# Turning the RWKV-7 recurrence's operands token-major: VectorE 32x32 block transposes in place of TensorE transposes through PSUM

## The chip, the cores and the metric

One Trainium2 chip, one core. The metric is the device time of the whole program in microseconds; three runs of the kernel before gave a median of 3381.07 us (3380.14 to 3383.0).

## What is computed

One decoder layer over 16 meta tokens and 2048 tokens of width 1024: a norm, one input projection, then two mixers side by side (sliding-window attention and an RWKV-7 recurrence), a gated merge, an output projection, and a SwiGLU feed-forward part. The change touches the recurrence alone. Cut to that:

```python
def step(S, inp):                       # per token, per head, state S is 64 x 64
    r_t, w_t, k_t, v_t, a_t, b_t = inp
    sa = einsum('bhvk,bhk->bhv', S, a_t)
    S = S * w_t[:, :, None, :] + sa[..., None] * b_t[:, :, None, :] + v_t[..., None] * k_t[:, :, None, :]
    y = einsum('bhvk,bhk->bhv', S, r_t)
    return S, y
```

The kernel computes this in chunks of 64 tokens, with the triangular system inside a chunk inverted.

## The kernel before, in words

**Two streams, one TensorE order.** The dense work is a generator: phase a (the input projection, 4 blocks of 512 tokens, 37 column chunks each) and then phase c for each block (branch projections `pb`, output projection `ph_o`, feed-forward products `pg`, `pu`, `ph_d`). Every product takes three matmul passes of 128x512 per 128 rows (`mm3`, a high and a low part of each operand). The mixers are generators too (`attn`, `lora`, `rwkv`). `tick()` advances one kind of mixer after every 4/3 us of dense work by a fixed credit, so each mixer moves one `yield` per 4 us of credit. `InOrder` (lines 82 to 98) ties all TensorE instructions to the order in which this loop writes them. On the other engines a scheduler places instructions by a timeline model; those of the dense part go through `High` (lines 191 to 206) and so take precedence. Three PSUM buffers (`psd`) serve the dense products, four (`psg`) the mixers, one (`psc`) the recurrence.

**One round of the recurrence.** `rwkv(i, j)` does 256 tokens (4 chunks) of 2 heads; there are 8 x 4 rounds and one more for the meta tokens, 33 in all. In order:
- The inputs are shifted into `rkv` (L562): r, k and v, feature-major. TensorE makes `pa` and `pz`; VectorE takes `rnb` (L679) and `kp` from `pa`.
- VectorE writes `bkd` (L730, L731): b and k of the four chunks, block-diagonal by head, 128 features by 128 (head, token). `bkd` has one buffer.
- TensorE multiplies `bkd` by `ar` into `pg` (this name is also used by the feed-forward gate; the mixer's is 128x128), VectorE masks it into `g` (L750, L756, L758).
- `g` goes through DRAM (`lt_d`) to GpSimd, which inverts the 32x32 blocks in 31 steps (L772, L774) into `xv`; that goes back through DRAM (`xt_d`) into `td`.
- Beside that inversion, L777 to L796 turn b, k (`bkd`) and v token-major: eight TensorE transposes into `pb`, two ScalarE copies into `bt`; two TensorE transposes of v into `pvv`, two VectorE and two ScalarE copies into the block-diagonal `vd`. (`pb` is also the name of the branch projections' PSUM tiles.)
- After `WAIT_INV` = 9 further yields `td` is read; VectorE turns its lower blocks (`tq`, L808, the kernel's only use of VectorE's transpose), and the four chunks run one after the other in the PSUM tile `ch`, with `vd`, `bt`, `ud` (L840), `rd` and the state `sd` (L845).

Up to three rounds are under way at once; a new one starts every 14 yields.

Of the kernel before, what the change touches and what calls it, by code (L numbers as in the profile page):

```python
# [19 lines left out]
F32 = mybir.dt.float32  # L20
F32R = mybir.dt.float32r
AF = mybir.ActivationFunctionType
# [5 lines left out]
P = 128  # L28
# [19 lines left out]
WAIT_INV = 9  # L48
# [30 lines left out]
def layer(ctx, tc, x, meta, w_in, w_br, w_o, w_gate, w_up, w_down, w2a, a2, g2, vecs, sinks, gfin,  # L79
          consts, rope, out):  # L80
    nc = tc.nc
    V, A, G, S = nc.vector, nc.scalar, nc.gpsimd, nc.sync
# [18 lines left out]
    T = InOrder()  # L101
# [8 lines left out]
    cp = pool("const")  # L110
    dp = pool("dram", space=DRAM)
    dn = pool("dense")
    mx = pool("mixer")
    psd = pool("psd", bufs=3, space=PSUM)
    psg = pool("psg", bufs=4, space=PSUM)
# [26 lines left out]
    ident = cc("ident")  # L142
# [407 lines left out]
    bkd = cp.tile([P, 2, 4, P], F32, name="bkd")  # L550
    vds = [cp.tile([P, 4, P], F32, name=f"vd{q}") for q in range(2)]
    td = cp.tile([P, 4, P], F32, name="td")
    rd = cp.tile([P, P], F32, name="rd")
    ud = cp.tile([P, P], F32, name="ud")
    for t in (bkd, *vds, td, rd):
        G.memset(t, 0.0)
    gmask = cst[:, _CC["gstrict"][0]:_CC["gincl"][1]]

# [56 lines left out]
    n = TU // CH  # L615

    def rwkv(i, j):
# [3 lines left out]
        m = i is None  # L621
        uid = 4 * NU if m else 4 * i + j
        nm = f"{i}_{j}"
        t1 = lambda s, b=1: mx.tile([P, TU], F32, tag=s, bufs=b, name=f"{s}_{nm}")
        cv = lambda ap: ap.rearrange("p (c t) -> p c t", t=CH)
# [17 lines left out]
        rm, km, vm = (rkv[:, q] for q in range(3))  # L643
# [84 lines left out]
        for h in range(2):  # L728
            hb = slice(64 * h, 64 * h + 64)
# [13 lines left out]
        for x in range(2):  # L743
            pg = psg.tile([P, 512], F32, tag="pg", name=f"pg_{nm}_{x}")
# [29 lines left out]
            G.tensor_add(xv[:, :, r + 1:], xv[:, :, r + 1:], pr[:, :, :n_])  # L774
        yield

        bt = mx.tile([P, 2, n, P], F32, tag="bt", bufs=2, name=f"bt_{nm}")  # L777
        vd = vds[(uid + m) % 2]
        for x in range(2):
            pb = psg.tile([P, 512], F32, tag="pg", name=f"pb_{nm}_{x}")  # L780
            for c in range(n):
                T.transpose(pb[:, c * P:(c + 1) * P], bkd[:, x, c], ident)
            A.activation(bt[:, x], pb.rearrange("p (c f) -> p c f", f=P), AF.Copy)
            if x == 0:
                yield
        pvv = psg.tile([P, 512], F32, tag="pg", name=f"pvv_{nm}")
        for t in range(2):
            T.transpose(pvv[:, t * P:(t + 1) * P], vm[:, t * P:(t + 1) * P], ident)
        pvt = pvv[:, :2 * P].rearrange("p (t f) -> p t f", f=P)
        for q in range(2):  # L790
            for h in range(2):
                hb, qb = slice(64 * h, 64 * h + 64), slice(64 * q, 64 * q + 64)
                if q == h:
                    V.tensor_copy(vd[hb, q::2, hb], pvt[qb, :, hb])
                else:
                    A.activation(vd[hb, q::2, hb], pvt[qb, :, hb], AF.Copy)  # L796
        for _ in range(WAIT_INV):
            yield
        G.dma_start(xt_d[uid].rearrange("m (b c) i -> b m (c i)", c=4), xv.rearrange("p c i -> p (c i)"))
        lo, hi = [slice(64 * h, 64 * h + 32) for h in range(2)], [slice(64 * h + 32, 64 * h + 64) for h in range(2)]  # L800
# [23 lines left out]
        for c in range(n):  # L824
# [8 lines left out]
            for h in range(2):  # L833
                hb = slice(64 * h, 64 * h + 64)
# [192 lines left out]
    def tick():  # L1027

        turn[0] = (turn[0] + 1) % TURNS
        rs = [u for u in units if u[2] == "r"]  # L1030
        for u in list(units):
            if turn[0] != (0 if u[2] == "a" else 1 if len(rs) > 1 and u is rs[0] else 2):
                continue
            u[1] += 1
            if next(u[0], 0) == 0:
                units.remove(u)
        if todo_r and turn[0] == 2:
            i, j = todo_r[0]
            b = (i or 0) // 2
            young = min((u[1] for u in units if u[2] == "r"), default=LAG)  # L1040
            if young >= LAG - 3 and i not in asked and set(range(6, 9)) <= emitted[b]:
                asked.add(i)
                start("l", lora(i), b)
            if young >= LAG and i in loras and set(
                    range(9, 21) if i is None else range(PAIR0 + 3 * j, PAIR0 + 3 * j + 3)) <= emitted[b]:
                todo_r.pop(0)
                start("r", rwkv(i, j), b)
        if todo_a and turn[0] == 0 and not any(u[2] == "a" for u in units):
            ti = todo_a[0]
            b = (ti or 0) // 4  # L1050
            if set(range(6)) <= emitted[b]:
                todo_a.pop(0)
                start("a", attn_meta() if ti is None else attn(ti), b)
# [135 lines left out]
```

## Time and profile before

| what | value |
|---|---|
| median of three runs | 3381.07 us |
| the profiled execution's own time | 3377.94 us |
| its span, first to last instruction | 3376.0 us |
| TensorE (PE) busy | 3256.3 us, 96% |
| VectorE (DVE) busy | 1542.1 us, 46% |
| ScalarE (ACT) busy | 1163.2 us, 34% |
| GpSimd (POOL) busy | 1156.1 us, 34% |
| mean granted TensorE clock | 0.987 |

The page's busy time is the union of an engine's instructions. The chain that ended last runs through PE for 60% of its span. Stages on the time axis: phase a to about 1150 us, phase c of the first block to about 1810 us, of the second to about 2370 us, of the third to about 2890 us, of the fourth to the end; the recurrence's rounds lie between about 190 and 2880 us. "Phase c" below means these stretches from 1150 us on.

### The profile page before, as it was taken

What the parts mean: (1) busy time and instruction counts of PE and PEld (TensorE: products, weight loads), DVE (VectorE), ACT (ScalarE), POOL (GpSimd) and SP (SyncE); (2) the same over time, 40 slices, a digit from 0 to 9 for tenths busy, and PEclk for the clock granted to TensorE, in tenths of its full rate; (3) what the DMA queues carried; (4) which work ended last, traced back from release to release, by engine and by line L of the source; (5) the groups of instructions that cost most, each with busy time, mean ns of one, the idle gap of its engine ahead of it and who ended that gap; (6) DMA issues with size and microseconds to landing.
All of it is one profiled execution on the core that took longest, in us unless ns stands there. A gap on an engine that the chain in (4) does not pass through costs nothing.

```text
span 3376.0 us, 47237 instructions
## 1 busy us (share of the span) xinstructions
PE 3256.3 (96%) x16909; PEld 2681.2 (79%) x16909; DVE 1542.1 (46%) x3622; ACT 1163.2 (34%) x2863; POOL 1156.1 (34%) x2771
## 2 busy tenths in 40 slices
PE   7899999999999998999999999999999999999998
PEld 6777887787888777887787788887888888778887
DVE  3343233232332585666666644445654443542233
ACT  4354344443443455445443422233242221220001
POOL 1124434334344454554453433444333341000000
PEclk9999999999999999999999999999999999999999
DMA  7777666676666776666668555556755555855555
GB/s 262 273 261 241 209 226 211 190 227 197 223 210 215 242 260 206 234 235 234 231 237 280 176 170 174 179 181 201 263 171 177 171 177 176 288 179 191 196 191 181
DMA packets 229448, 721.46 MB, mean 214 GB/s; under 512 B 36333, under 2 KB 90989, under 8 KB 168286
## 3 DMA queue, kind: packets, MB, share of 16 engines
q1 hardware_dynamic: 158126, 516.15, 47.1%
q0 software_dynamic: 38736, 154.99, 12.9%
q10 hardware_dynamic: 32352, 47.31, 3.8%
q8 instruction: 133, 2.18, 0.3%
q14 instruction: 101, 0.83, 0.1%
HBM read 533.46 MB, written 184.82 MB: 213 GB/s over the span
## 4 chain that ended last, share of the span: by engine, by line
PE 60%; DMA 6%; DVE 3%; POOL 3%; ACT 2%; issue 2%; SPq 0%; POOLq 0%; DVEq 0%; ACTq 0%
PE pg L93 14%; PE pu L93 12%; PE ph_d L93 11%; PE pi L93 6%; PE pb L93 4%; PE ch L93 4%; PE ph_o L93 3%; DMA yl<-y_d 1%; PE ph_o_l L93 1%; POOL pr L772 1%; POOL xv L774 1%; DMA lt<-lt_d 1%; PE py L93 1%; PE pq L93 1%; DVE h L202 1%
## 5 line engine op out<-in xcount | busy, mean ns | idle before, releaser
L93 PE MATMUL pi<-act_u,w_in 128*128 128x512 f32 x3552 | 902.5, 402 | 10.5 <-DVE m L202 6.1
L93 PEld LDWEIGHTS pi<-act_u,w_in 128*128 128x128 f32 x3552 | 652.9, 191 | 144.0 <-issue 5.5
L93 PE MATMUL pg<-act_f,w_g 128*128 128x512 f32 x2112 | 533.7, 399 | 6.8 <-DVE act_f L202 6.8
L93 PE MATMUL pu<-act_f,w_u 128*128 128x512 f32 x2112 | 522.9, 395 | 0.0
L93 PE MATMUL ph_d<-w_d,mg_g 128*128 128x512 f32 x1920 | 472.5, 397 | 10.4 <-DVE h L202 10.0
L93 PEld LDWEIGHTS pg<-act_f,w_g 128*128 128x128 f32 x2112 | 388.4, 189 | 85.3 <-DVE act_f L202 9.0
L93 PEld LDWEIGHTS pu<-act_f,w_u 128*128 128x128 f32 x2112 | 388.9, 188 | 78.8 <-issue 1.0
L93 PEld LDWEIGHTS ph_d<-w_d,mg_g 128*128 128x128 f32 x1920 | 355.5, 189 | 85.9 <-DVE h L202 14.5
L772 POOL TENSOR_TENSOR pr<-xv,lt 128x124 f32<-128x124 f32 (+30 forms) x992 | 330.5, 333 | 248.9 <-DMA lt<-lt_d 176.8
L774 POOL TENSOR_TENSOR xv<-xv,pr 128x124 f32<-128x124 f32 (+30 forms) x992 | 341.1, 344 | 74.5
L202 DVE SCALAR_TENSOR_TENSOR h<-ph_d,h 128x512 f32<-128x512 f32 x320 | 218.9, 689 | 130.0 <-PE ph_d L93 128.3
L93 PE MATMUL pb<-ya,w_br 128*128 128x512 f32 x768 | 191.0, 400 | 1.0 <-DMA w_br<-wd_br 0.6
L93 PEld LDWEIGHTS pb<-ya,w_br 128*128 128x128 f32 x768 | 143.1, 191 | 30.9 <-DVE mg_m L202 1.0
L202 DVE SCALAR_TENSOR_TENSOR th<-th,pg 128x512 f32<-128x512 f32 x88 | 60.4, 687 | 214.6 <-ACT th L202 214.5
L93 PE MATMUL ph_o<-w_o,mg_m 128*128 128x512 f32 x576 | 144.2, 400 | 6.8 <-DVE h L202 3.8
L804 POOL DMA_DIRECT2D td<-xt_d x132 | 72.6, 557 | 225.4 <-PE ch L93 197.3
L202 ACT ACTIVATE th<-pg 128x512 f32<-128x512 f32 x88 | 52.6, 598 | 281.4 <-PE pg L93 281.0
L202 DVE TENSOR_TENSOR th<-th,pu 128x512 f32<-128x512 f32 x88 | 60.5, 687 | 183.8 <-PE pu L93 183.3
L243 POOL TENSOR_TENSOR ss_o<-ss_o,mhalf 128x1 f32<-128x1 f32 x16 | 9.4, 590 | 372.5 <-DVE ss_o L202 372.3
L755 POOL DMA_DIRECT2D lt_d<-g x128 | 71.2, 561 | 184.0 <-DVE g L750 182.0
L202 ACT ACTIVATE mg_g<-th 128x512 fp32r<-128x512 f32 x88 | 55.3, 628 | 222.6 <-DVE th L202 222.5
L93 PEld LDWEIGHTS ph_o<-w_o,mg_m 128*128 128x128 f32 x576 | 106.5, 190 | 31.3 <-DVE h L202 5.2
(356 smaller groups left out, 4512.1 us busy)
## 6 DMA issues: line engine op xcount, KB each, us to landing
w_in<-wd_in SPq DMA_DIRECT2D x111, 1024.0 KB, 5.5
w_g<-wd_g SPq DMA_DIRECT2D x66, 1024.0 KB, 5.0
w_u<-wd_u SPq DMA_DIRECT2D x66, 1024.0 KB, 5.0
w_d<-wd_d SPq DMA_DIRECT2D x60, 1024.0 KB, 5.0
wd_in<-w_in POOLq DMA_DIRECT2D x37, 1024.0 KB, 5.8
w_br<-wd_br SPq DMA_DIRECT2D x24, 1024.0 KB, 7.0
wd_g<-w_g POOLq DMA_DIRECT2D x22, 1024.0 KB, 5.2
wd_u<-w_u POOLq DMA_DIRECT2D x22, 1024.0 KB, 5.3
```

Of the source, the lines that this page charges most:

```text
L93: r = f(*p, **k)
L202: return f(*p, **k)
L243: G.tensor_tensor(ss[:rows, 3:4], ss[:rows, 2:3], mhalf[:rows, 0:1], op=ALU.pow)
L755: G.dma_start(lt_d[uid, m0:m0 + n].rearrange("c j i -> j c i"), g[r32, :, 0, o])
L772: G.tensor_mul(pr[:, :, :n_], xv[:, :, r:r + 1].to_broadcast([P, 4, n_]), lt[:, r, r + 1:].unsqueeze(1).to_broadcast([P, 4, n_]))
L774: G.tensor_add(xv[:, :, r + 1:], xv[:, :, r + 1:], pr[:, :, :n_])
L804: G.dma_start(td[r32, :, r32], xt_d[uid, m0:m0 + 4].rearrange("m j i -> j m i"))
```

## The change

The ten TensorE transposes of a round, its two 128x512 ScalarE copies from PSUM and its four copies of v go. In their place VectorE issues 24 transposes of 32 partitions by 4 blocks of 32, from SBUF straight into SBUF: eight from v into the diagonal blocks of `vd`, sixteen from `bkd` into the diagonal blocks of `bt`. `bt` becomes two fixed tiles that GpSimd zeroes once at the start; it was a rotating pair before, so the space is the same. The number of yields of a round stays: 1 + 9 before, 2 + 8 now. Half of the new transposes (r different from q) write to other partitions than they read.

```diff
-    for t in (bkd, *vds, td, rd):
+    bts = [cp.tile([P, 2, 4, P], F32, name=f"bt{q}") for q in range(2)]
+    for t in (bkd, *vds, td, rd, *bts):
         G.memset(t, 0.0)
...
-        bt = mx.tile([P, 2, n, P], F32, tag="bt", bufs=2, name=f"bt_{nm}")
-        vd = vds[(uid + m) % 2]
+        bt, vd = bts[(uid + m) % 2], vds[(uid + m) % 2]
+        vc4 = cv(vm)
+        for h in range(2):
+            for r in range(2):
+                for q in range(2):
+                    rb, qb = (slice(64 * h + 32 * z, 64 * h + 32 * z + 32) for z in (r, q))
+                    V.transpose(vd[qb, :, rb], vc4[rb, :, 32 * q:32 * q + 32])
         for x in range(2):
-            pb = psg.tile([P, 512], F32, tag="pg", name=f"pb_{nm}_{x}")
-            for c in range(n):
-                T.transpose(pb[:, c * P:(c + 1) * P], bkd[:, x, c], ident)
-            A.activation(bt[:, x], pb.rearrange("p (c f) -> p c f", f=P), AF.Copy)
-            if x == 0:
-                yield
-        pvv = psg.tile([P, 512], F32, tag="pg", name=f"pvv_{nm}")
-        for t in range(2):
-            T.transpose(pvv[:, t * P:(t + 1) * P], vm[:, t * P:(t + 1) * P], ident)
-        pvt = pvv[:, :2 * P].rearrange("p (t f) -> p t f", f=P)
-        for q in range(2):
+            yield
             for h in range(2):
-                hb, qb = slice(64 * h, 64 * h + 64), slice(64 * q, 64 * q + 64)
-                if q == h:
-                    V.tensor_copy(vd[hb, q::2, hb], pvt[qb, :, hb])
-                else:
-                    A.activation(vd[hb, q::2, hb], pvt[qb, :, hb], AF.Copy)
-        for _ in range(WAIT_INV):
+                for r in range(2):
+                    for q in range(2):
+                        rb, qb = (slice(64 * h + 32 * z, 64 * h + 32 * z + 32) for z in (r, q))
+                        V.transpose(bt[qb, x, :, rb], bkd[rb, x, :, qb])
+        for _ in range(WAIT_INV - 1):
             yield
```

**Where the instructions stand, PE.** One round in phase c of the first block, among the passes of an output projection (`ph_o`) and of a branch projection (`pb_6_0`, with `ya` and `w_br`). Before:

```order
L93 MATMUL ph_o_5_1_1_11952<-w_o_5_1_11933,mg_m_3_11374 128x512 x3
L93 MATMUL ch_2_0_11783<-rd,td 128x128
L93 MATMUL pb_3_0_11962<-cst,bkd 128x128 x4
L93 MATMUL ph_o_5_2_1_11969<-w_o_5_1_11933,mg_m_2_11304 128x512 x3
...
L93 MATMUL pb_6_0_12008<-ya_1_11083,w_br_6_11997 128x512 x3
L93 MATMUL pb_3_1_12015<-cst,bkd 128x128 x4
L93 MATMUL pvv_3_12021<-cst,rkv_3_11340 128x128 x2
L93 MATMUL pb_6_0_12008<-ya_2_11089,w_br_6_11997 128x512 x3
```

With the change:

```order
L93 MATMUL ph_o_5_1_1_12004<-w_o_5_1_11985,mg_m_3_11426 128x512 x3
L93 MATMUL ch_2_0_11835<-rd,td 128x128
L93 MATMUL ph_o_5_2_1_12022<-w_o_5_1_11985,mg_m_2_11356 128x512 x3
...
L93 MATMUL pb_6_0_12061<-ya_1_11127,w_br_6_12050 128x512 x3
L93 MATMUL pb_6_0_12061<-ya_2_11133,w_br_6_12050 128x512 x3
```

The ten transposes of the round are gone and everything else stands in its place; the same holds for all 33 rounds, 330 instructions.

**DVE, behind bkd.** The same round, from its last `bkd` product on (`mt`: a branch projection leaves PSUM; `w_br`: low part of a weight; `kw`: attention keys; `gst`: the norm of an earlier round). Before:

```order
L731 TENSOR_TENSOR bkd<-kp_3_11489,pi_3_11635 64x4x64
L202 SCALAR_TENSOR_TENSOR mt_5_0_11670<-tg_5_0_11605,pb_5_0_11620 128x512
L859 TENSOR_REDUCE gst_1_11679<-ysq_1_11683 128x4
L736 TENSOR_TENSOR fc_3_11651<-pe_3_11633 128x3
L822 TENSOR_SCALAR sd_110<-sd_110,pe_2_3_11654 128x128
L885 TENSOR_TENSOR kw<-kl_11744,kw 64x128 x4
L202 SCALAR_TENSOR_TENSOR mt_5_1_11707<-tg_5_1_11607,pb_5_1_11672 128x512
L860 TENSOR_SCALAR gst_1_11679<-gst_1_11679 128x4
L202 TENSOR_TENSOR w_br_6_11997<-wr_br_6_0_11998,w_br_6_11997 128x512
```

With the change:

```order
L737 TENSOR_TENSOR fc_3_11703<-pe_3_11685 128x3
L818 TENSOR_SCALAR sd_110<-sd_110,pe_2_3_11706 128x128
L792 STREAM_TRANSPOSE bt_122<-bkd 32x4x32
L881 TENSOR_TENSOR kw<-kl_11796,kw 64x128 x2
L792 STREAM_TRANSPOSE bt_122<-bkd 32x4x32 x4
L881 TENSOR_TENSOR kw<-kl_11796,kw 64x128 x2
L792 STREAM_TRANSPOSE bt_122<-bkd 32x4x32
L202 SCALAR_TENSOR_TENSOR mt_5_1_11759<-tg_5_1_11659,pb_5_1_11724 128x512
L792 STREAM_TRANSPOSE bt_122<-bkd 32x4x32
L856 TENSOR_SCALAR gst_1_11731<-gst_1_11731 128x4
L792 STREAM_TRANSPOSE bt_122<-bkd 32x4x32
```

The sixteen transposes into `bt` stand right behind `bkd`, between the dense instructions and ahead of `g` (L751 in the changed kernel).

**DVE, behind rkv.** The same round earlier, among the products that add an output projection to `h`. Before:

```order
L202 SCALAR_TENSOR_TENSOR h_11105<-ph_o_3_0_1_11459,h_11105 128x512
L202 TENSOR_TENSOR w_br_5_11609<-wr_br_5_1_11614,w_br_5_11609 128x512
L202 SCALAR_TENSOR_TENSOR h_11105<-ph_o_3_1_1_11467,h_11105 128x512
L679 TENSOR_SCALAR rnb_3_11500<-pa_3_11487 64x2 x4
L602 MEMSET dl_12191 64x256
```

With the change:

```order
L202 SCALAR_TENSOR_TENSOR h_11149<-ph_o_3_0_1_11511,h_11149 128x512
L202 TENSOR_TENSOR w_br_5_11661<-wr_br_5_1_11666,w_br_5_11661 128x512
L785 STREAM_TRANSPOSE vd_117<-rkv_3_11392 32x4x32 x8
L202 SCALAR_TENSOR_TENSOR h_11149<-ph_o_3_1_1_11519,h_11149 128x512
L680 TENSOR_SCALAR rnb_3_11552<-pa_3_11539 64x2 x4
```

The eight transposes into `vd` stand ahead of the sum that frees the next PSUM buffer and ahead of `rnb`; in 28 of the rounds the eight stand together.

## Rows read from the trace of the kernel before

**Rows 1.** The page, part 1: busy us, share of the span, instructions

```profile
PE 3256.3 (96%) x16909; PEld 2681.2 (79%) x16909; DVE 1542.1 (46%) x3622; ACT 1163.2 (34%) x2863; POOL 1156.1 (34%) x2771
```

**Rows 2.** Busy time by stretch: PE, PEld, DVE, ACT, POOL, then clock, DMA share, GB/s

```profile
0.00:1150.00 1150.00, 1093.60 (x5842) 893.12 (x5843) 390.41 (x1164) 482.56 (x1184) 401.17 (x971) 0.98 0.69 226
1150.00:1810.00 660.00, 625.88 (x3296) 509.85 (x3295) 445.32 (x1017) 318.61 (x788) 334.32 (x715) 0.98 0.70 239
1810.00:2370.00 560.00, 552.50 (x2957) 461.14 (x2956) 281.83 (x623) 165.00 (x425) 231.00 (x606) 0.99 0.59 192
2370.00:2890.00 520.00, 515.01 (x2751) 431.13 (x2750) 245.11 (x541) 133.17 (x345) 174.60 (x460) 0.99 0.56 187
```

**Rows 3.** Waits of PE: us in total, times, longest us

```profile
PE psS L93 <- DVE qs L956: 27.3, 9, 5.8
...
PE ph_d L93 <- DVE h L202: 10.0, 7, 4.5
```

**Rows 4.** Timeline of PE, 320 to 328 us: start us, us, instructions

```profile
320.35 1.63 PE L93 MATMUL pi<-act_u,w_in 128*128 128x512 f32 x6
321.82 0.60 PE L93 MATMUL pb<-cst,bkd 128*128 128x128 f32 x4
322.17 3.02 PE L93 MATMUL pi<-act_u,w_in 128*128 128x512 f32 x12
...
325.17 1.63 PE L93 MATMUL pi<-act_u,w_in 128*128 128x512 f32 x6
...
327.07 0.38 PE L93 MATMUL pvv<-cst,rkv 128*128 128x128 f32 x2
327.21 1.17 PE L93 MATMUL pi<-act_u,w_in 128*128 128x512 f32 x4
```

**Rows 5.** The chain that ended last, a dense run without mixers

```profile
3084.14 10.88 PE ph_d L93 x48
```

**Rows 6.** Groups by shape: busy us, mean ns, then idle before and its releaser

```profile
L93 PE MATMUL pb<-cst,bkd 128*128 128x128 f32 x256 | 38.8, 275 | 0.0
...
L783 ACT ACTIVATE bt<-pb 128x512 f32<-128x512 f32 x64 | 38.2, 596 | 120.9 <-PE pb L93 120.9
...
L794 DVE COPY vd<-pvv 64x128 f32<-64x128 f32 x64 | 18.4, 288 | 26.8 <-ACT vd L796 15.1 <-PE pvv L93 10.8
...
L93 PE MATMUL pvv<-cst,rkv 128*128 128x128 f32 x64 | 12.2, 273 | 0.0
```

**Rows 7.** The tile tq: duration ns min/median/max, first and last start

```profile
L808 DVE STREAM_TRANSPOSE tq<-td x64: 289/302/304, 385.0 to 2815.8; 32x128 f32<-32x128 f32 x64
```

**Rows 8.** Timeline of DVE, 459 to 461 us: two transposes in a row

```profile
459.16 0.62 DVE L808 STREAM_TRANSPOSE tq<-td 32x128 f32<-32x128 f32 x2
```

**Rows 9.** DVE busy from bkd's end to g, eight rounds, 1150 to 1810 us

```profile
1213.76:1220.11 6.35, 6.28 (x16) 1.00 0.69 169
...
sum 59.32, DVE 36.77; mean DVE 4.60
```

**Rows 10.** The same, thirteen rounds, 1810 to 2890 us

```profile
sum 94.90, DVE 40.90; mean DVE 3.15
```

**Rows 11.** The same, twelve rounds before 1150 us

```profile
sum 111.01, DVE 22.44; mean DVE 1.87
```

**Rows 12.** Waits of ACT and DVE: us in total, times, longest us

```profile
ACT bt L783 <- PE pb L93: 120.9, 48, 6.8
...
DVE g L750 <- PE pg L93: 74.3, 26, 7.4
```

**Rows 13.** Timeline of PE, 1536 to 1552 us: the longest wait for h

```profile
1542.80 2.93 PE L93 MATMUL ph_d<-w_d,mg_g 128*128 128x512 f32 x6 [4.52 <-DVE h L202]
```

**Rows 14.** PE busy behind that wait: us, busy, granted clock, DMA share, GB/s

```profile
1542.80:1545.50 2.70, 2.70 (x6) 0.50 0.60 241
```

**Rows 15.** Timeline of POOL, the start of the program

```profile
1.31 0.94 POOL L556 MEMSET bkd<- 128x1024 f32 x1
...
6.43 0.58 POOL L243 TENSOR_TENSOR ss_a<-ss_a,mhalf 128x1 f32<-128x1 f32 x1 [1.06 <-DVE ss_a L202]
```

## The prediction

> **What bounds the kernel now.** Read the page's shares first [rows 1]: PE is busy for 96% of the span, and the next engine, DVE, for 46%. So PE sets the time, and work taken off PE is worth its own length unless PE then waits. A share over the whole span hides stages, so the busy time by stretch comes next [rows 2]: in phase a PE lacks 56 us of 1150, in phase c of the first block 34 of 660, and in the next two stretches only 7.5 of 560 and 5 of 520. DVE fills 34%, 67%, 50% and 47% of the four. The first block of phase c is the place where DVE is short of time: there it also makes the low parts of the weights. Third, who makes PE wait [rows 3]: DVE, for attention's split of q (27.3 us, at the end of a GpSimd chain) and for the sums into h (10.0 us). PE lacks 119.7 us in all. DVE is thus the engine that can take back what PE gains.
>
> **PE, what goes.** 330 transposes leave an otherwise unchanged order. Their price is not the 270 ns of one, since matmuls overlap; it is how far they push the next dense pass. A dense pass takes 10.88 / 48 = 0.2267 us [rows 5]. Six passes that start at 320.35 should give way at 320.35 + 1.36 = 321.71; the next begins at 322.17, so four transposes cost 0.46 us [rows 4]. From 325.17, six passes and six transposes: 327.21 - 325.17 - 1.36 = 0.68 us [rows 4]. A round loses 1.14 us of PE, and 33 rounds 37.6 us. The other bound is the union of their busy time, 38.8 + 12.2 = 51.0 us for 32 rounds [rows 6], 52.6 for 33; but a transpose's last part lies under the next pass, so I take 37.6. The rows put one transpose in a run at 0.11 us. The Trainium skill (VectorE: DVE Perf Modes, "The three transpose paths") gives 390 ns for a 128x128 bf16 transpose on TensorE; an estimate by that figure of the skill would be 330 x 0.39 = 129 us gone, and the spacing in the trace disagrees with it by more than three times, as these stand in runs.
>
> **ACT, what goes.** Two copies of 0.596 us a round [rows 6], 39 us in all, and two small ones; and ACT no longer stands idle in its queue for `pb`, 120.9 us [rows 12]. PE hardly ever waits on ACT, so I count this at nothing; it is cover for DVE, which often follows ACT. From below it can be a few us of gain.
>
> **DVE, what comes.** The one transpose of the kernel has the same shape, 32 partitions by 128 elements: 0.302 us [rows 7], two in a row 0.62, so 0.31 each [rows 8]. 24 of them are 7.4 us a round, 33 rounds 245 us; the two copies of v that go are 2 x 0.288 us a round [rows 6], 19 us. DVE rises by 226 us to some 1768, 52% of the span. In the first block of phase c, with 8 rounds in 660 us, it goes from 445 to 500 us, 76%. No row shows a transpose whose output lies on other partitions than its input, as half of the new ones have: I bound it by 0.29 (the copy of v, which is about as large) and 0.60 us (ACT's copy of four times the elements [rows 6]) and take 0.31, since shape and engine are the same.
>
> **What of it lies beside other work.** The results are wanted ten yields later, over 40 us, so no one waits for `bt` or `vd` themselves. What counts is who stands behind them in DVE's queue. The sixteen of `bt` (5.0 us) run between `bkd` and `g`. In the twelve rounds of phase a that gap has 111.0 - 22.4 = 88.6 us of idle DVE for 12 x 5.0 = 59.5 us of transposes [rows 11]: hidden. In the eight rounds of the first phase c block it has 59.3 - 36.8 = 22.5 us for 39.7 [rows 9]; the worst one, at 1213.76, has 0.07 us idle of 6.35. There 17.1 us do not fit. In the thirteen later rounds 54.0 us are idle for 64.5 [rows 10]: 10.5 do not fit. Together 27.6 us of DVE work is pushed back in phase c. Behind it stand two sorts of instructions: those that free a PSUM buffer for PE (`mt`, `h`, `th`), which the order puts between the transposes, so that they wait for one or a few of them, and `g`, whose user is the inversion. The bounds of what reaches PE are 0 and all 27.6 us; between them I take half, 14 us, because the dense instructions are let in between and PE has three buffers to run on with. The eight of `vd` (2.5 us) go in a gap where DVE waits for `pa`; in the row order they stand ahead of a sum into `h`, and I count that within the same 14.
>
> **The start.** GpSimd zeroes two more tiles of the size of `bkd`, 0.94 us each, ahead of the norm's first power, where it has 1.06 us idle [rows 15]: up to 0.8 us later, and that only for the first of four row tiles. Nothing.
>
> **The sum.** 37.6 - 14 = 23.6 us less. From the profiled execution's 3377.94 us that gives 3354.3; the median of the runs is 3.1 us above that execution, so 3357 us.
>
> **Rivals.**
> 1. *All of it is kept*: the dense work let in between the transposes is on time, PE waits no more than now. For: the order interleaves them wherever the queue is full, and in the last three stretches PE waits so little that it has much slack in buffers. Against: 27.6 us that do not fit. 3381.1 - 37.6 = 3343.5 us.
> 2. *PE waits for the rest of the chain instead*: its long waits end on GpSimd and DMA chains (q through the rotary product, `td` through DRAM), which do not get shorter. A round in which PE waits anyhow gives back its 1.14 us; with some 13 such rounds that is 15 us, and with 22 us of stalls behind DVE nothing is left: 3381 us, no change.
> 3. *Slower: DVE's bursts stall PE and its clock falls.* A wait of 4.52 us for a sum into h [rows 13] was followed by 2.70 us at a granted clock of 0.50 [rows 14], the lower of the two levels (1.2 of 2.4 GHz): half of that, about 1.4 us, is lost on top of the wait. If all 27.6 us reach PE and each of the 21 rounds of phase c pays 1.4 us more, that is 57 us: 57 - 37.6 = 19 us slower, 3400 us. It decides from 37.6 / 21 = 1.8 us lost per round of phase c. A transpose of 0.60 us across partitions would bring it there alone. For: a DVE that was 99% busy in the worst gap; 24 small instructions where 2 stood. Against: the dense instructions take precedence. The Trainium skill speaks for this rival (same page, "The TRN2 errata"): each instruction that reads SBUF pays a fixed latency, so many small tiles pay it many times, and its rules advise TensorE for a full 128x128 transpose if PSUM will do. By that rule the change should lose on DVE; the trace agrees on the price, 302 ns for 128 elements a partition against 288 ns for the copy of v, but cannot say whether DVE's time counts.
>
> **How the numbers follow.** Part of the gain kept (3357): 0.53. All of it (3343.5): 0.15. Nothing left (3381): 0.14. Slower (3400): 0.18. A measurement of this kernel can tell about 0.2%, 6.8 us, from no change, so below 3374 is faster, above 3388 slower: 0.68 faster, 0.14 the same, 0.18 slower. The range reaches below the full gain by a few us for ACT's relief, to 3340, and up half way into the slower case, to 3390: some 5% lie below it and 12% above. The likeliest case alone lies between 3343.5 (no stall) and 3371 (all 27.6 us).
>
> **What would show it.** Right: PE's instructions fall by 330 and PE busy by about 38 to 50 us; two transposes in a row at 0.31 us, across partitions too; DVE busy near 1768 us, ACT near 1105; PE's idle time up from 120 us by some 14, on waits for DVE's `h`, `mt`, `act_f` and `qs`, most of it from 1150 to 1810 us; `g` some us later behind `bkd`. Wrong: a transpose across partitions well over 0.31 us; PE's idle unchanged or less (rival 1); new PE waits for `tq` or `td` (rival 2); DVE over 85% of the first phase c block and low clock in many gaps there (rival 3).

## The result, and the profile after

| | before | after |
|---|---|---|
| median of four runs each | 3380.61 us (3372.07 to 3383.0) | 3405.2 us (3400.42 to 3412.59) |
| ratio, 95% interval | | 1.0083 [1.0061, 1.0105] |
| the profiled execution's own time | 3377.94 us | 3412.59 us |
| its span | 3376.0 us | 3410.8 us |
| PE busy + PE idle in the span | 3256.3 + 119.7 us | 3244.2 + 166.6 us |
| mean granted TensorE clock | 0.987 | 0.978 |

The change makes the kernel 0.83% slower: 28 us by the ratio, 24.6 us between the two medians. The forecast was 3357 us, faster; the time lies above its range. The profiled execution of the changed kernel is the longest of its four, so the traces below lie 34.8 us apart, more than the runs do.

The page of the changed kernel, part 1, answers to [rows 1]:

```profile
PE 3244.2 (95%) x16579; PEld 2661.1 (78%) x16579; DVE 1757.7 (52%) x4348; ACT 1112.4 (33%) x2731; POOL 1160.5 (34%) x2773
```

PE has lost its 330 instructions but only 12.1 us of busy time, at a lower clock, and its idle time rose by 46.9 us. That is the whole difference of the two spans: 46.9 - 12.1 = 34.8 us. By stretch, with the borders again at the first branch projection of each block (columns as in [rows 2]):

```profile
0.00:1157.00 1157.00, 1091.27 (x5725) 888.59 (x5726) 470.47 (x1428) 462.69 (x1136) 406.07 (x974) 0.97 0.68 224
1157.00:1823.00 666.00, 613.46 (x3141) 495.52 (x3141) 482.64 (x1145) 303.47 (x742) 325.88 (x709) 0.96 0.66 230
1823.00:2392.00 569.00, 548.64 (x2908) 456.13 (x2907) 334.85 (x807) 153.74 (x400) 230.44 (x599) 0.99 0.59 191
2392.00:2941.00 549.00, 536.27 (x2812) 447.01 (x2811) 301.27 (x708) 134.52 (x346) 186.17 (x478) 0.99 0.58 191
```

From border to border the stages took 1150.4, 640.9, 568.3 and 545.9 us before and take 1157.1, 665.9, 569.4 and 548.5 us now. The first block of phase c pays 25 us of it; there PE lacks 52.5 us, at a clock of 0.96. Phase a, where all was forecast to be hidden, pays 6.7 us. In the last two stretches the gain of PE and the loss nearly cancel.

The transposes themselves (groups by shape, columns as in [rows 6]) cost what [rows 7] said, also where the output lies on other partitions, as half of them do; all 792 lie between 289 and 310 ns:

```profile
L792 DVE STREAM_TRANSPOSE bt<-bkd 32x128 f32<-32x128 f32 x528 | 159.6, 302 | 7.9
```

Waits of PE in the changed kernel, answering to [rows 3]; after them two lines of before that the rows did not show:

```profile
PE psS L93 <- DVE qs L952: 32.3, 9, 7.1
PE ph_d L93 <- DVE h L202: 12.9, 9, 2.9
PE pq L93 <- DVE tq L804: 12.2, 3, 5.0
PE py L93 <- ACT ptt L998: 10.8, 6, 4.3
PE ph_o L93 <- DVE h L202: 6.1, 5, 1.8
```

```profile
PE pq L93 <- DVE tq L808: 6.9, 2, 5.2
...
PE py L93 <- ACT ptt L1002: 4.8, 2, 3.3
```

All waits for a sum into `h`, over every PSUM tile, went from 15.5 to 25.5 us; those for `tq`, which end the way through GpSimd's inversion, from 6.9 to 12.2 us. These two make up 15 of the 47 us. The rest is spread over a dozen others, `ptt` with 6.0, `yt` with 5.1 and `qs` with 5.0 us at their head; no chain carries it alone, and no wait for `tq` lies in the first block of phase c, where most is lost. One round of the first phase c block shows how they come about. DVE's timeline (start, length, instructions):

```profile
1669.08 0.68 DVE L202 SCALAR_TENSOR_TENSOR h<-ph_d,h 128x512 f32<-128x512 f32 x1
1669.68 2.50 DVE L792 STREAM_TRANSPOSE bt<-bkd 32x128 f32<-32x128 f32 x8
1672.21 0.69 DVE L202 SCALAR_TENSOR_TENSOR h<-ph_d,h 128x512 f32<-128x512 f32 x1
...
1680.26 0.41 DVE L751 TENSOR_TENSOR g<-pg,rnb 128x256 f32<-128x256 f32 x1
```

and PE's at the same place:

```profile
1672.96 1.65 PE L93 MATMUL ph_d<-w_d,mg_g 128*128 128x512 f32 x6 [1.03 <-DVE h L202]
...
1675.83 1.95 PE L93 MATMUL pg<-ar,bkd 128*128 128x128 f32 x16
...
1681.15 0.49 PE L93 MATMUL psS<-kw,qs 128*128 128x272 f32 x2 [1.62 <-DVE g L757]
```

Eight transposes stand between two sums into `h`; the sum at 1672.21 releases a PSUM buffer that PE waits 1.03 us for. And `pg` is done by about 1677.8, but `g` starts at 1680.26: eight more transposes and what was let in between them stand ahead of it. PE waits 1.62 us for `g`, and behind `g` stands the whole inversion. Averaged over 32 rounds, worked out from the timelines, `g` starts 1.17 us after `pg` does before the change and 1.86 us after it, 3.26 us in the first block of phase c.

The eight of v hold DVE in another way. They write one of the two `vd` tiles, which the chunks (`ch`) of an earlier round may still be reading; drawn forward as they are, they wait for that at the head of DVE's queue, 16 times, of which 7 with 20.7 us lie in phase a. DVE's waits in the changed kernel:

```profile
DVE vd L785 <- PE ch L93: 35.7, 16, 5.6
```

In e6 below, where they stand behind `g`, these waits are gone.

### The profile page after: what moved, and what is told of

Read it like the earlier page. It is cut to its first block, busy times and chain, and to the rows that moved or that the text cites. A ratio compares the mean times of both kernels' runs of the same rounds, so it can differ in the third digit from the quotient of the medians.

```text
span 3410.8 us, 47182 instructions
## 1 busy us (share of the span) xinstructions
PE 3244.2 (95%) x16579; PEld 2661.1 (78%) x16579; DVE 1757.7 (52%) x4348; ACT 1112.4 (33%) x2731; POOL 1160.5 (34%) x2773
## 4 chain that ended last, share of the span: by engine, by line
PE 43%; DVE 5%; DMA 4%; POOL 2%; issue 1%; ACT 1%; SPq 0%; POOLq 0%; DVEq 0%; ACTq 0%
PE pg L93 12%; PE pu L93 11%; PE ph_d L93 10%; PE pb L93 3%; PE ch L93 2%; PE ph_o L93 2%; DVE h L202 1%; DMA w_o<-wd_o 1%; DMA lt<-lt_d 1%; DVE bt L792 1%; POOL xv L775 1%; POOL pr L773 1%; DMA wr_d<-in_w_down 1%; DMA yl<-y_d 1%; PE pq L93 0%
## 5 line engine op out<-in xcount | busy, mean ns | idle before, releaser
L93 PEld LDWEIGHTS pi<-act_u,w_in 128*128 128x128 f32 x3552 | 659.9, 192 | 145.6 <-issue 5.5
L93 PEld LDWEIGHTS ph_d<-w_d,mg_g 128*128 128x128 f32 x1920 | 355.1, 189 | 89.4 <-DVE h L202 17.8
L792 DVE STREAM_TRANSPOSE bt<-bkd 32x128 f32<-32x128 f32 x528 | 159.6, 302 | 7.9
L857 POOL TENSOR_TENSOR gst<-gst,mhalf 128x4 f32<-128x4 f32 x32 | 33.9, 1059 | 347.8 <-DVE gst L856 329.9
```

What stands on the lines that cost most here:

```text
L93: r = f(*p, **k)
L792: V.transpose(bt[qb, x, :, rb], bkd[rb, x, :, qb])
L857: G.tensor_tensor(st[:, 3], st[:, 2], mhalf[:, 0:4], op=ALU.pow)
```

## The experiments

Each kernel was timed against the kernel before on the same chip; the experiments lie on four chips, so they are compared by their ratios. A hundredth of a per cent is about 0.34 us. By the intervals, a difference of two ratios is clear of noise from some 0.2% on (7 us), against the change itself from 0.3%. A trace shows one execution, which lies up to 17 us from its kernel's median, so waits that differ by a few us between two traces tell little by themselves. Apart from the transposes, TensorE's instructions run in the same order in the traces of all the kernels. `late(...)` (line 103 of the changed kernel) ties an instruction to its place in the written order; without it, as in the change, the scheduler draws the sixteen transposes of `bkd` forward, ahead of `g`.

| run | transposes on DVE | ratio to the kernel before, 95% interval |
|---|---|---|
| after | as changed | 1.0083 [1.0061, 1.0105] |
| e1 | none at all | 0.9950 [0.9933, 0.9967] |
| e2 | as changed, PE's ten kept | 1.0167 [1.0147, 1.0187] |
| e4 | b, k as changed; v on TensorE | 1.0051 [1.0033, 1.0068] |
| e5 | v alone; b, k on TensorE | 1.0007 [0.9993, 1.0021] |
| e3 | 24 behind `g`, three per yield | 0.9971 [0.9955, 0.9987] |
| e8 | e3, each issued twice | 1.0009 [0.9997, 1.0021] |
| e6 | 24 behind `g`, runs of eight | 0.9960 [0.9945, 0.9976] |
| e12 | e6, PE's ten kept | 1.0018 [1.0005, 1.0031] |
| e11 | 24 behind `g`, runs of four | 0.9988 [0.9974, 1.0001] |
| e13 | 24 behind `g`, b and k in a run of sixteen | 1.0007 [0.9992, 1.0022] |
| e7 | 24 behind `g` in one run | 1.0045 [1.0029, 1.0062] |
| e9 | v's eight ahead of `g`, sixteen behind | 0.9986 [0.9970, 1.0003] |
| e14 | b's eight ahead, sixteen behind | 1.0001 [0.9988, 1.0014] |
| e10 | b's and k's sixteen ahead, v's eight behind | 1.0074 [1.0061, 1.0087] |
| e15 | e6, `g` one yield later | 1.0092 [1.0069, 1.0114] |

**What the two halves are worth: e1 and e2.** e1 takes all turning out; e2 is the changed kernel with PE's transposes back in, into PSUM tiles that nobody reads.

```diff
 e1: for x in range(2):
         yield
-        for h ... V.transpose(bt[qb, x, :, rb], bkd[rb, x, :, qb])
-    for h ... V.transpose(vd[qb, :, rb], vc4[rb, :, 32 * q:32 * q + 32])
 e2: V.transpose(bt[qb, x, :, rb], bkd[rb, x, :, qb])
+    pb = psg.tile([P, 512], F32, tag="pg", name=f"pb_{nm}_{x}")
+    for c in range(n):
+        T.transpose(pb[:, c * P:(c + 1) * P], bkd[:, x, c], ident)
+    ... (and the two of v into pvv)
```

> Leaves out the turning of b, k and v altogether: no TensorE transposes, no ScalarE or VectorE copies of them, and no VectorE transposes (bt stays zero, vd stays zero). It prices what PE and ACT get back with nothing added on DVE. Queue theory (PE's 38 us are real, and DVE's 24 transposes a round cost some 62 us through PE's waits and clock): 3381 - 38 = about 3343 us. Wait theory (PE then waits earlier for GpSimd and DMA chains, so the 38 us were never to be had): 3365 to 3381. Reshuffling theory (any change of the order loses time here): near 3400.

> The changed kernel with TensorE's ten transposes a round kept, into PSUM tiles that nobody reads (no copies). DVE works as in the change, PE as before. Queue theory: PE's 38 us come on top of the changed kernel, 3405 + 38 = about 3443 us, and the difference to the kernel before, some 62 us, is what DVE's transposes cost. Wait theory: PE's work fits into the waits, 3405 to 3415.

e1 gained 0.50%, 17 us, where 37.6 had been counted for PE's part. So with no new work on DVE at all, and the copies on ACT and DVE gone as well, about half of the forecast gain is missing. From e1 to the change is 1.33%, 45 us: that is what the 24 transposes on DVE cost, more than the 27.6 us that the prediction had as their upper bound. From the change to e2 is 0.84%, 28 us, for PE's ten transposes. The page of e1:

```profile
PE 3230.5 (96%) x16579; PEld 2656.1 (79%) x16579; DVE 1520.2 (45%) x3556; ACT 1110.6 (33%) x2731; POOL 1161.9 (34%) x2773
```

and among its waits

```profile
PE psS L93 <- DVE qs L941: 39.3, 9, 8.6
```

PE's busy time did fall, by 25.8 us, at a clock of 0.982 against 0.987. The span of 3373.3 us leaves 142.8 us idle, 23 more than before, and the wait for `qs` alone grew from 27.3 to 39.3 us: PE comes sooner to what is not ready sooner. But this is e1's longest execution, 3375.08 us where the median of eleven is 3357.6 us; it shows the way in which PE's gain is lost, not how much of it. e12 and e6, further down, are the better pair for that.

**Which of the operands: e4 and e5.** In e4 v stays on TensorE, in e5 b and k do.

```diff
 e4 (from the change):
-    V.transpose(vd[qb, :, rb], vc4[rb, :, 32 * q:32 * q + 32])
+    T.transpose(pvv[:, t * P:(t + 1) * P], vm[:, t * P:(t + 1) * P], ident)
+    ... (and the four copies from pvv)
 e5 (from the kernel before):
-    T.transpose(pvv[:, t * P:(t + 1) * P], vm[:, t * P:(t + 1) * P], ident)
-    ... (and the four copies from pvv)
+    V.transpose(vd[qb, :, rb], vc4[rb, :, 32 * q:32 * q + 32])
```

> b and k on DVE as in the change (16 transposes a round), v on TensorE with its four copies as before. Load theory: two thirds of DVE's cost, 41 us, against 31 us from eight of ten PE transposes: 3391 us. If the eight of v hurt most (they stand ahead of the sums into h and of the start of the round's chain): about 3360. If the sixteen hurt most (they delay g and the inversion): about 3400.

> v on DVE as in the change (8 transposes a round in one run), b and k on TensorE with their two copies as before. So far all 24 in long runs lost 45 us against no turning at all, and the 16 of b and k with v left on TensorE lost 17 us against the kernel before. If costs add up: a little above the kernel before, by some 5 to 10 us (8 of the 24 cost 15, two PE transposes give some 5 back). If the run of v ahead of the sums into h is the worse one: over 15 us slower. If only the 16 hurt: 0 to 5 us faster.

The loss sits mostly with b and k; moving v, with TensorE's two transposes and the four copies of v gone, changes nothing that can be measured.

**The same work in another place: e3, e6, e7, e8, e11.** All 24 are pinned behind `g`. e6 is the changed kernel with nothing but `late(...)` around each transpose; in e3, e11 and e7 they come as three at each of eight yields, four at each of six, and all at one; e8 is e3 with each issued twice. The yields of a round stay the same.

```diff
 e6:
-    V.transpose(vd[qb, :, rb], vc4[rb, :, 32 * q:32 * q + 32])
+    late(V.transpose(vd[qb, :, rb], vc4[rb, :, 32 * q:32 * q + 32]))
-    V.transpose(bt[qb, x, :, rb], bkd[rb, x, :, qb])
+    late(V.transpose(bt[qb, x, :, rb], bkd[rb, x, :, qb]))
 e3 (e11: range(6), 4 * s, then 4 yields; e7: two yields, all 24, then 8 yields):
+    for s in range(8):
+        yield
+        for x, h, r, q in turns[3 * s:3 * s + 3]:
+            late(V.transpose(...))
+    for _ in range(2):
+        yield
```

> The changed kernel with the 24 transposes of a round held in program order on DVE, three at each of eight yields, in place of runs of 8 and up to 16; the number of yields is the same. DVE's sum of work is unchanged. If the length of a run ahead of the instructions that PE waits for is what costs (burst theory): most of the 62 us go, 3350 to 3365 us. If DVE's sum of time costs wherever it stands (load theory): about 3400, as the changed kernel.

> The changed kernel with each run of eight transposes held in program order: on DVE they then stand behind the round's g, in runs of eight one yield apart, not ahead of it. Same yields, same work. Place theory (what cost 38 us was that the runs stand ahead of g and of what follows from it): as the spread form, 0.995 to 1.000 of the kernel before. Length theory (any run of 2.5 us and more ahead of what frees PE's buffers costs): between the spread form and the change, 1.002 to 1.008.

> All 24 transposes of a round in one place, held in program order behind g, two yields after the start of the inversion; same number of yields. Place theory: as the spread form, up to 1.002 of the kernel before. Length theory: a run of 7.4 us is worse than the change's 5.0 and 2.5: 1.008 or more.

> The spread form with every transpose issued twice (six at each of eight yields; the second writes the same again), so DVE has 245 us more. It prices DVE's time by itself. The spread form's 24 a round cost about 9 us against no turning at all (0.9971 against 0.995). If DVE's time is cheap as long as it is spread: 10 to 15 us more, about 1.000 to 1.002 of the kernel before. If its sum counts with a threshold in the first block of phase c: 30 us and more, 1.006 or above.

> All behind g, in runs of four at six yields in place of eight at three. Length theory (2.5 us in a run still costs something): below 0.996, by up to 0.002. If a run of 2.5 us is already short enough: 0.996, the same.

e6 is 1.23% faster than the change, with the same instructions in another order on DVE, and 0.40% faster than the kernel before. It stands 0.10% behind e1, which turns nothing, less than the runs can tell apart: placed like this, 24 transposes are almost free. e8 says the same of DVE's time as such: 24 more a round, 239 us of DVE's busy time, cost 0.38%, 13 us. e7 loses 0.85% on e6 by the length of the run; at 1.0045 it lies between its two expectations. Its longest wait of PE, and DVE's timeline ahead of it:

```profile
1237.68 1.65 PE L93 MATMUL ph_o<-w_o,mg_m 128*128 128x512 f32 x3 [6.53 <-DVE h L202]
```

```profile
1222.06 2.51 DVE L788 STREAM_TRANSPOSE vd<-rkv 32x128 f32<-32x128 f32 x8
1224.58 2.83 DVE L790 STREAM_TRANSPOSE bt<-bkd 32x128 f32<-32x128 f32 x9
...
1230.97 0.94 DVE L790 STREAM_TRANSPOSE bt<-bkd 32x128 f32<-32x128 f32 x3
...
1232.91 1.48 DVE L950 TENSOR_TENSOR qs<-q,qs 64x512 fp32r<-64x512 f32 x1
...
1236.94 0.68 DVE L202 SCALAR_TENSOR_TENSOR h<-ph_o,h 128x512 f32<-128x512 f32 x1
```

7.5 us of transposes within ten push back everything behind them, and five more us of other work come first; the sum into `h` that PE needs is the last of the row, and PE stands 6.53 us. Over e7 PE waits 41.8 us for `h`, in e6 16.1 us, before the change 15.5 us. The waits of e7:

```profile
PE ph_d L93 <- DVE h L202: 26.6, 17, 4.1
PE ph_o L93 <- DVE h L202: 9.2, 3, 6.5
PE pq L93 <- DVE tq L802: 6.4, 2, 5.4
```

and of e6:

```profile
PE psS L93 <- DVE qs L952: 33.2, 9, 8.5
PE ph_d L93 <- DVE h L202: 10.5, 15, 2.6
PE pq L93 <- DVE tq L804: 8.5, 2, 4.3
```

e11's runs of four met neither expectation: they came out between e3 and e13 rather than beside e6 or below it. Runs shorter than eight are thus no gain by themselves, and why four at six yields lose 0.28% to eight at three was not found.

**Place against length: e9, e10, e13, e14.** Part of the 24 unpinned, as in the change, the rest pinned behind `g`; e13 has b's and k's sixteen in one run behind `g`.

```diff
 e9, v ahead:       only the bt transposes become late(...)
 e10, b and k ahead: only the vd transposes become late(...)
 e14, b ahead:      vd's and those with x == 1 become late(...)
 e13:
+    yield
+    yield
     for x in range(2):
-        yield
         for h ... late(V.transpose(bt[qb, x, :, rb], bkd[rb, x, :, qb]))
```

> The eight transposes of v stand as in the change (ahead of the round's first operations and of sums into h), the sixteen of b and k are held in program order behind g. All 24 behind g gave 0.996, the change 1.0083: 1.2% between them, some 41 us. Place theory, with the sixteen as its larger part (27 of the 41 us by their number): 0.999 to 1.001. If all the cost lies with the sixteen ahead of g: 0.996 again. If it lies with the eight of v: near 1.008.

> The other half: the sixteen of b and k stand as in the change, right behind bkd and ahead of g; the eight of v are held behind g. Place theory by numbers: 1.003 to 1.005. If all the cost lies with the sixteen: near 1.008. If it lies with the eight of v: 0.996.

> v's eight behind g; the sixteen of b and k in one run of 5 us, also behind g, where the form at 0.996 has two runs of eight. The same sixteen ahead of g gave 1.0074. If the place ahead of g is what costs: 0.996 to 0.999. If the run's length is: 1.003 to 1.007.

> Only the eight of b stand ahead of g, as one run of 2.5 us right behind bkd; v's and k's eights stand behind g as in the form at 0.996. If the place costs by the number that stands there: half way, 1.002. If it is a run that no longer fits into DVE's idle time between bkd and g (5.0 us into 1.7 to 4.2 us in the mean of phase c's stretches): a run of 2.5 us fits nearly, 0.996 to 0.999.

Against e6, sixteen behind `g` in one run cost 0.47%, 16 us; eight ahead of `g` 0.41%, 14 us; sixteen ahead 1.14%, 38 us; v's eight 0.26%, 9 us. v's eight and the sixteen, 0.26% and 1.14%, add up to about the 1.23% between e6 and the change. Both place and length count; e13 and e14 lie between the two expectations of each. With the number held, e10 against e13, the place costs 0.67%, 23 us. Some of the waits behind it, e10, sixteen ahead of `g`:

```profile
PE pq L93 <- DVE tq L804: 12.1, 3, 4.9
...
PE pyt L93 <- DVE yt L858: 4.9, 1, 4.9
```

e13, sixteen in a run behind it:

```profile
PE ph_d L93 <- DVE h L202: 16.6, 14, 3.0
PE pq L93 <- DVE tq L805: 7.5, 2, 4.4
```

A long run shows as waits for `h` (27.1 us in all in e13, 23.9 in e10, 16.1 in e6). Sixteen ahead of `g` show in part as waits for `tq` (12.1 us in e10; 7.5 and 8.5 in e13 and e6) and in part elsewhere: e10 has a wait of 4.9 us for `yt`, the output of an earlier round, that e13 does not have, and 8.4 us more on `qs` and `act_u`. That the place costs is shown; that it costs by making `g` late is not. In e10 `g` starts 1.94 us after `pg` does, in e13 1.14 and in e6 1.24 us. But in e14 it starts no later than in e6, 1.23 us, and the eight ahead of it cost 14 us all the same, with waits for `h` at 24.8 us.

**What is kept of PE's gain: e12.** e6 with PE's ten transposes put back unread, as in e2.

> The form behind g in runs of eight, with TensorE's ten transposes kept into PSUM tiles that nobody reads. It prices PE's ten transposes where DVE is in good order. Spacing theory: PE's 38 us in full, so 0.996 + 0.011 = 1.007. If part of PE's time only moves into waits for other chains, as in the kernel without any turning (17 us of 38): 1.001 to 1.003.

0.58% against e6, 20 us: PE's part is worth 17 us (e1), 20 us here, and 28 us in the change's own order (e2). The three cannot be told apart by their intervals. e12's page, and its wait for `qs`:

```profile
PE 3257.4 (97%) x16909; PEld 2677.7 (79%) x16909; DVE 1746.6 (52%) x4348; ACT 1109.2 (33%) x2731; POOL 1161.3 (34%) x2773
...
PE psS L93 <- DVE qs L958: 26.2, 9, 5.3
```

Against e6's trace that is 28.7 us more of busy time (3228.7 us there) and 17.8 us less idle, 115.4 against 133.2 us. So between these two traces most of what PE gains goes into waits, 7.0 us of it into the one for `qs`.

**`g` late by itself: e15.** e6 with the three products of `g` written one yield later and pinned, one yield fewer behind, and the transposes still behind `g`.

```diff
+    yield
     for x in range(2):
-        V.tensor_mul(g[:, :, 0], ...
+        late(V.tensor_mul(g[:, :, 0], ...
...
-    for _ in range(WAIT_INV - 1):
+    for _ in range(WAIT_INV - 2):
```

> The form at 0.996 with g itself one yield (about 4 us) later and held in program order, one yield less afterwards, so that the chunks start at the same yield; no transpose stands ahead of it. If what costs is that g, and with it the inversion through DRAM and GpSimd, comes late: 1.003 or more. If it is the dense and attention instructions that stand behind a long run: 0.996 to 0.999.

1.32% slower than e6, 45 us, without any transpose ahead of `g`. Lines of its waits:

```profile
POOL td L809 <- PE ch L93: 72.2, 15, 11.2
...
PE pq L93 <- DVE tq L813: 16.4, 4, 8.2
```

PE waits twice as long for `tq` as in e6, and GpSimd's write of `td`, which in e6 waited 177.2 us in all for its buffer, now waits 72.2: the slack behind the inversion is what a late `g` uses up. But here `g` starts 7.37 us after `pg` does, 6.1 us later than in e6, where the change makes it 0.7 us later than before. The edit also holds the PSUM buffers of `pg` a yield longer and shifts other instructions, and waits for `h` rose to 35.9 us. So it shows that a late `g` can cost, at some nine times the delay of the change; it does not show what share of the change's loss that is.

**A rival that fell.** In every variant the scheduler moved other instructions as well. If the amount of that reshuffling were the cause, time would follow it. In the order of the traces, with what the change takes out or puts in left aside, 141 of DVE's 3556 other instructions stand elsewhere than before in the changed kernel and 85 in e6. But e3 and e9, with 105 and 128, are at 0.9971 and 0.9986, and e10, with 99, at 1.0074. That a few of the moved instructions matter more than their number is not ruled out.

## Why the prediction was wrong, point by point

- **PE bounds, DVE can take it back**: right, and the reason the sign was open.
- **330 instructions go**: right. **PE's 37.6 us in full**: wrong. By e1 and e12 they are worth 17 to 20 us. The price of 1.14 us a round may well stand, as PE's busy time fell by 26 to 29 us in the traces; the rest of the gain turned into waits for chains that did not get shorter (from e12 to e6 17.8 us more idle, 7.0 of them for `qs`) and into a clock of 0.984 against 0.987 there. That is rival 2, which was put at 15 us and left out of the sum. It should have been a term of the sum: it holds in every case, not in one.
- **ACT's relief worth nothing**: not separated. ACT fell to 1112.4 us, as forecast (1105).
- **0.31 us a transpose, across partitions too; DVE 1768 us**: right, 302 ns, 2.50 us for eight, and 1757.7 us.
- **Hidden in phase a, 27.6 us pushed back in phase c, half of it reaching PE**: the step that failed. It took DVE's idle time between `bkd` and `g` as what the transposes cost, 27.6 us at most, and halved that; 45 us were paid. That idle time says nothing of where the transposes stand and in what runs. With the same 24 and the same order on TensorE, e6 costs 0.10% against none at all and the change 1.33%; sixteen in one run behind `g` cost 16 us, sixteen ahead of it 38. Phase a was to hide them: it took 1150.4 us before, 1157.1 in the change and 1141.8 in e6, and PE waits for no sum into `h` there that could explain it. The prediction named `g` as pushed back, and then priced it with the dense instructions; the runs show that a place ahead of `g` costs, and leave open by which wait.
- **The eight of `vd` within the same 14 us**: 9 us by e9 against e6, on top. The prediction asked who stands behind them, not what they wait for themselves: a `vd` tile still in use, 35.7 us at the head of DVE's queue in the changed kernel and 35.3 in e9. How much of the 9 us comes from that is not shown.
- **The start, nothing**: in the trace of after GpSimd reaches the norm's first power at 7.28 us against 6.43 [rows 15], close to the 0.8 us that was named.
- **Where it shows**: the first phase c block and its low clock, as rival 3 said; its sign was right, and its time, 3400 us, near. Its terms were both too large, 57 us lost against 45 and 37.6 gained against 17, and partly cancel, so that its time came near by luck. One of its signs did not come: DVE was to be over 85% busy in that block and was 72%, 482.6 us of 666. Its point of decision, 1.8 us lost per round of phase c, was too high for the same reason: with 17 us gained, 0.8 us per round decide.
- **302 ns beside 288 ns**: the copy of v that rival 3 sets beside the transpose reads PSUM, the transpose reads SBUF, so the two do not show what a read from SBUF costs.
- **The weights**: 0.18 for that rival rested on "the dense instructions take precedence". That precedence lets a dense instruction in between two transposes; it does not move the transposes behind `g`.

The Trainium skill (VectorE: DVE Perf Modes, "Rules for kernel authors") would leave a 128x128 transpose on TensorE where PSUM will do. For the order of the change the measurement agrees, 1.0083; for e6, the same instructions in another place, it does not, 0.9960. What decides here is not the engine's price of a transpose.

**What beats both kernels**: e6, 3364.55 us median, ratio 0.9960 [0.9945, 0.9976], the change with the transposes pinned behind `g`.

**What stays open**: how the 38 us of the sixteen divide between `g`, `h` and the other waits. e10 against e13 gives 23 us for the place, but e10's run is broken up by dense instructions and e13's mostly is not, and e14 pays for the place without a later `g`.

## What to carry to other kernels

Work moved to an engine with half its time free is priced by who stands behind it in that engine's queue: find the head of a long chain (here `g`) and the instructions that free the bounding engine's buffers (here `h`), and place the new work behind the one and in runs that do not hold up the other (here eight, not sixteen or 24). Ask also what the new work itself waits for, since it holds the queue meanwhile. Of time taken off the bounding engine count only what is left after the waits that it will reach sooner; here about half. And pin new work whose result is wanted late, since a scheduler may draw it forward.

## What was not expected of the hardware

VectorE's transpose of 32 partitions by 128 fp32 elements takes 302 ns whether or not its output lies on the partitions of its input. And TensorE's granted clock was lower in the kernels in which it stood idle most: 0.987 at 119.7 us idle (before), 0.984 at 133.2 (e6), 0.978 at 166.6 (after). So part of the loss lies in busy time: after and e6 have the same PE instructions in the same order, and after's are busy for 15.5 us more. The sum of idle time does not fix the clock, though: e7 had 0.985 at 155.8 us, e5 0.983 at 127.4.
